# One run of heads beside one run of projections: a two-layer attention trunk with its groups joined

## The chip, the core and the metric

The kernel runs on one core of a Trainium2 chip. The metric is the device time of one execution in microseconds (us); the kernel before took 1171.78 us (median of three runs, 1171.17 to 1171.89). Engines are named as the profile names them: PE multiplies matrices, PEld loads its weights, DVE is the vector engine, ACT the scalar engine, POOL the general one, and SP issues most transfers.

## The reference

The input is 512 tokens of 1024 numbers, float32. There are two layers. Cut to what matters here:

```python
h = rms_norm(x, g_mix[0])
proj = h @ w_in_even             # A: q, k, v of 8 heads; B: q of 8 heads, k and v of 2
a_out = dilated_attention(aq, ak, av, slopes)               # strided windows, three dilations
b_out = sliding_window_sink_attention(bq, bk, bv, sinks, slopes)   # window 128, learned sink
x = x + concat(a_out, b_out) @ w_out_even
x = x + squared_relu_mlp(rms_norm(x, g_mlp[0]), w_up[0], w_down[0])
h = rms_norm(x, g_mix[1])
proj = h @ w_in_odd              # q, k, v of 16 heads C, and a forget logit per head
x = x + forgetting_attention(q, k, v, log_f) @ w_out_odd
x = x + squared_relu_mlp(rms_norm(x, g_mlp[1]), w_up[1], w_down[1])
```

Queries and keys are normed per head (`rms_norm` over 64 numbers). Every head is a causal softmax attention with a bias on the logits.

## The kernel before, in words

**Precision.** Each product of two float32 matrices is made of three matmuls, with both operands split into a high and a low half (`whi`, `wlo` for weights). The split costs an instruction on ACT, POOL or DVE for the high half and one on DVE or POOL for the low half, per 128 x 512 weights.

**Projections.** `project` multiplies the normed input with 256 or 512 columns of the input weights. It runs over the 8 blocks of 128 input rows and the 4 blocks of 128 tokens: 96 matmuls into the four `pj` banks of PSUM (tag `pA`). Then a callback uses the banks. For values `prep_v` scales and splits them. For queries and keys `norm_heads` (L240 to L261) copies each bank (ACT, L247), squares it (ACT, L249), sums by head (DVE, L250), takes a reciprocal root in some 15 small DVE instructions, and multiplies two tiles on DVE and two on POOL (L260). `project` is a generator: it yields after every 12 matmuls, and each yield counts as 64 columns where 512 are projected, 32 where 256 are.

**Heads.** `attend` goes over pairs of heads. For a pair, `prep_q` and `prep_k` transpose the normed tiles on PE (`qkT`, L267) and split them (ACT and DVE, L277, L278, L159, L160); the second half of each K is filled by a transfer that SP issues (L290). `scores` makes four blocks of scores per head (`S`, L325, L326), biases them and takes the row extreme (DVE, L339), exponentiates (ACT, L342) and scales by the reciprocal sum (POOL, or ACT for the last block). `values` transposes the probabilities (`PT`, L362), splits them (ACT L374, DVE L375), multiplies with V (`O`, L382) and adds halves (`yf`, ACT L385, DVE L386). The values of a head are made during the scores of the next one. All these banks share the four of tag `pB`. The generator yields after each block, so that a pair of heads is 19 steps, 14 for the first pair of a layer.

**Output projection.** `out_part` multiplies finished pairs of heads (`ys`) with the output weights (`op`, 12 matmuls and one DVE addition per 128 columns for four pairs). The last two pairs' part is done at the start of the MLP stage, by `finish`.

**What sets the order.** `run` (L430) takes one generator of heads and one of projections and steps the one that lags: projections go when their share of `n_dense` columns is not above the heads' share of `n_att` steps plus a lead. Layer 0 has three such runs: the first four dilated heads (0 to 3) beside the projections of the sliding-window heads; the eight sliding-window heads (4 to 11) beside the projections of the second dilated group; heads 12 to 15 beside two thirds of the output projection. Layer 1 has four runs, of heads 16 to 19, 20 to 23, 24 to 27 and 28 to 31, beside the next group's projections and at last the output projection. `LEADS` holds a lead for each run: 0, 0, -0.16 in layer 0, and 0.33, -0.3, -0.23, -0.09 in layer 1. A run ends only when both of its generators are done. This order is the order of recording; a scheduler then turns it into the order of each engine, moving ready instructions ahead within limits.

## Time and profile before

| | |
|---|---|
| median of three runs | 1171.78 us |
| the profiled execution | 1169.99 us, span 1168.2 us |
| first score of head 0, head 4, head 12, head 15 | 54.22, 107.66, 172.25, 199.03 us |
| first `up` matmul of layer 0's MLP | 227.79 us |
| first score of head 16, head 31 | 627.40, 802.67 us |
| first `up` matmul of layer 1's MLP | 831.05 us |

The profile is of one execution, so its times are compared with its own 1169.99 us, not with the median. Busy time of PE counts every matmul's modelled duration, and these overlap: a matmul of 512 columns is shown with 0.39 us and the next one starts 0.23 us after it. So a wait of PE is best seen as a start that comes late. The granted clock of PE was 1.00 in all stretches that are used here. POOL works in the attention stages alone.

### The profile page before, as it was taken

To read this page: it belongs to the slowest core of one execution; us is meant where nothing else is said; L and a number is where in the kernel's file an instruction comes from. 1 tells how busy PE (TensorE), PEld (TensorE's weight loads), DVE (VectorE), ACT (ScalarE), POOL (GpSimd) and SP (SyncE) were. 2 spreads that over 40 slices of the span, in tenths; PEclk is the share of its full clock that TensorE was granted. 3 is DMA by queue.
4 is the path that set the end of the run, shared out by engine and by line. 5 is a ranking of instruction groups with operands and counts; after the bars stand their busy time and mean duration, and the time that the engine had idled before them with its cause. 6 is when DMAs were issued, how large, how long until landed. Compare 5 with 4: busy or idle time off the path is not lost.

```text
span 1168.2 us, 17496 instructions
## 1 busy us (share of the span) xinstructions
PE 1146.4 (98%) x6256; PEld 981.4 (84%) x6256; DVE 879.8 (75%) x1870; ACT 646.6 (55%) x1349; POOL 203.0 (17%) x296
## 2 busy tenths in 40 slices
PE   8999989999999999999999999999999999999998
PEld 7987878887988988988887888888888888888887
DVE  7878999969947847855647877788858749669676
ACT  6556867655445545444335685656756455465452
POOL 1445434200000000000155445332100000000000
PEclk9999999999999999999999999999999999999999
DMA  7532024132332332333443323343430721623403
GB/s 257 160 91 73 19 73 145 58 123 73 101 117 91 91 108 91 96 121 108 148 127 109 103 89 110 100 124 112 163 106 3 232 91 51 202 73 108 148 34 109
DMA packets 100655, 126.57 MB, mean 108 GB/s; under 512 B 6184, under 2 KB 79944, under 8 KB 100568
## 3 DMA queue, kind: packets, MB, share of 16 engines
q1 hardware_dynamic: 99384, 121.23, 34.0%
q10 hardware_dynamic: 608, 2.13, 0.5%
q0 software_dynamic: 576, 2.10, 0.4%
q8 instruction: 49, 0.80, 0.3%
q14 instruction: 38, 0.31, 0.1%
HBM read 112.29 MB, written 6.32 MB: 102 GB/s over the span
## 4 chain that ended last, share of the span: by engine, by line
PE 82%; DVE 9%; DMA 3%; ACT 2%; POOL 1%; issue 1%; SPq 0%; ACTq 0%; POOLq 0%; DVEq 0%
PE up L164 10%; PE up L167 10%; PE up L168 10%; PE pj L231 4%; PE pj L233 4%; PE pj L232 4%; PE O L382 3%; PE PT L362 2%; PE Y L1023 2%; PE Y L1022 2%; PE Y L1020 2%; PE op L168 2%; PE op L164 2%; PE op L167 2%; PE S L325 2%; DVE wlo L155 1%
## 5 line engine op out<-in xcount | busy, mean ns | idle before, releaser
L164 PE MATMUL up<-xin,whi 128*128 128x512 f32 x512 | 200.5, 392 | 0.0
L168 PE MATMUL up<-xin,whi 128*128 128x512 f32 x512 | 199.3, 389 | 0.0
L167 PE MATMUL up<-xin,wlo 128*128 128x512 f32 x512 | 199.2, 389 | 0.0
L769 ACT CAST whi<-wraw 128x512 fp32r<-128x512 f32 x228 | 139.2, 619 | 105.5 <-PE up L168 47.3
L770 DVE TENSOR_TENSOR wlo<-wraw,whi 128x512 fp32r<-128x512 f32 x228 | 151.7, 686 | 53.7 <-ACT whi L769 53.5
L168 PEld LDWEIGHTS up<-xin,whi 128*128 128x128 f32 x512 | 96.1, 188 | 20.1
L164 PEld LDWEIGHTS up<-xin,whi 128*128 128x128 f32 x512 | 96.1, 188 | 19.9 <-issue 0.2
L167 PEld LDWEIGHTS up<-xin,wlo 128*128 128x128 f32 x512 | 96.2, 188 | 19.7 <-issue 0.2
L342 ACT ACTIVATE P<-P,negm 128x128 f32<-128x128 f32 (+5 forms) x128 | 69.6, 544 | 51.8 <-DVE negm L339 47.9
L231 PE MATMUL pj<-whi,hn 128*128 128x512 f32 (+2 forms) x256 | 88.7, 346 | 0.0
L951 ACT ACTIVATE u<-up 128x512 f32<-128x512 f32 x64 | 38.3, 598 | 90.9 <-PE up L168 90.9
L233 PE MATMUL pj<-whi,hn 128*128 128x512 f32 (+2 forms) x256 | 86.9, 339 | 0.0
L232 PE MATMUL pj<-wlo,hn 128*128 128x512 f32 (+2 forms) x256 | 86.8, 339 | 0.0
L152 POOL TENSOR_SCALAR whi<-wraw 128x512 fp32r<-128x512 f32 x88 | 61.1, 696 | 141.5 <-PE pj L233 121.3
L790 DVE TENSOR_TENSOR t<-u 128x256 f32<-128x256 f32 x56 | 23.2, 424 | 63.3 <-ACT u L1094 61.5
L155 POOL TENSOR_TENSOR wlo<-wraw,whi 128x512 fp32r<-128x512 f32 x48 | 64.4, 1345 | 20.8 <-ACT whi L150 18.1
L231 PE MATMUL pj<-whi,h 128*128 128x512 f32 (+1 forms) x192 | 65.6, 348 | 0.7 <-DVE v L160 0.7
L232 PE MATMUL pj<-wlo,h 128*128 128x512 f32 (+1 forms) x192 | 65.3, 341 | 0.2 <-DVE wlo L155 0.2
L233 PE MATMUL pj<-whi,h 128*128 128x512 f32 (+1 forms) x192 | 65.5, 343 | 0.0
L350 POOL TENSOR_SCALAR P<-P,rden 128x256 f32<-128x256 f32 (+2 forms) x96 | 47.7, 500 | 90.8 <-DVE rden L345 90.1
L155 DVE TENSOR_TENSOR wlo<-wraw,whi 128x512 fp32r<-128x512 f32 (+1 forms) x72 | 49.7, 697 | 17.5 <-POOL whi L152 9.8
L374 ACT CAST PT<-PT 128x256 fp32r<-128x256 f32 (+3 forms) x128 | 49.5, 405 | 19.3 <-PE PT L362 18.5
(229 smaller groups left out, 3051.7 us busy)
## 6 DMA issues: line engine op xcount, KB each, us to landing
wraw<-in_w_up SPq DMA_DIRECT2D x64, 512.0 KB, 4.0
wraw<-in_w_down SPq DMA_DIRECT2D x56, 512.0 KB, 4.2
wraw<-in_w_in_odd SPq DMA_DIRECT2D x36, 256.0 KB, 3.4
mraw<-in_w_down SPq DMA_DIRECT2D x16, 512.0 KB, 4.7
K<-K SPq DMA_DIRECT2D x26, 256.0 KB
wraw<-in_w_in_even SPq DMA_DIRECT2D x10, 512.0 KB, 4.0
wraw<-in_w_in_even SPq DMA_DIRECT2D x16, 256.0 KB, 4.5
xl<-xsp SPq DMA_DIRECT2D x8, 512.0 KB
```

The source lines that it names most:

```text
L152: nc.gpsimd.tensor_scalar(dst_h, src, 1.0, 1.0, op0=OP.mult, op1=OP.mult)
L155: in_order((nc.gpsimd if lo == "pool" else nc.vector).tensor_sub(dst_l, src, dst_h.bitcast(F32)))
L164: m = nc.tensor.matmul(o, wh, xh, start=start, stop=False, skip_group_check=more)
L167: nc.tensor.matmul(o, wl, xh, start=False, stop=False, skip_group_check=more)
L168: nc.tensor.matmul(o, wh, xl, start=False, stop=stop, skip_group_check=more)
L231: nc.tensor.matmul(o, xh, hi[:, :n], start=k == 0, stop=False)
L232: nc.tensor.matmul(o, xh, lo[:, :n], start=False, stop=False)
L233: nc.tensor.matmul(o, xl, hi[:, :n], start=False, stop=k == DC - 1)
L342: nc.scalar.activation(p[:, :ne], p[:, :ne], AF.Exp, scale=-1.0, bias=negm[:, i:i + 1], accum_out=den[:, i:i + 1])
L374: nc.scalar.copy(dst[:, 0], pt[:, :n])
L769: sca(nc.scalar.copy(dst_h, src))
L770: late.append(lambda: vec(nc.vector.tensor_sub(dst_l, src, dst_h.bitcast(F32))))
```

## The change

`run` now takes the heads of a whole layer as one generator and all its projections, with the first parts of the output projection behind them, as another. In place of a share and a lead it has a list of points (heads' steps, projected columns); between points the wanted number of columns is a straight line, and projections go while they are below it. `LEADS`, `NB`, `AHEAD` and `ahead` are gone. `SKEW` is 200: at the end of each group of heads the projections stand 200 columns beyond the point that the group needs; at step 0 they stand 100 columns ahead.

```diff
-LEADS = (0.0, 0.0, -0.16, 0.33, -0.3, -0.23, -0.09)
+SKEW = 200
-NB = 86
@@
-            def run(att, n_att, dense, n_dense, lead=0.0):
+            def run(att, dense, points):
                 a = d = 0
-                while True:
-                    if d / n_dense <= (a + lead * n_att) / n_att or att is None:
+                while att is not None:
+                    (a0, d0), (a1, d1) = next((p, q) for p, q in zip(points, points[1:]) if a < q[0] or q is points[-1])
+                    if dense is not None and d < d0 + (d1 - d0) * (a - a0) / (a1 - a0):
                         c = next(dense, None)
                         if c is None:
-                            break
-                        d += c
+                            dense = None
+                        else:
+                            d += c
+                    elif next(att, "end") == "end":
+                        att = None
                     else:
-                        if next(att, "end") == "end":
-                            att = None
                         a += 1
-                if att is not None:
-                    for _ in att:
+                if dense is not None:
+                    for _ in dense:
                         pass
@@
-                run(att_a(0), 32, chain(kv_b(), project([(1536, 2048)], qk_use("b", 8))), 768, LEADS[0])
-                run(att_b(), NB, chain(qk_a(1), v_a(1)), 768, LEADS[1])
-                run(chain(att_a(1), last_values()), 38, chain(out_part([0, 1, 4, 5], True),
-                                                              out_part([6, 7], False), ahead([2, 3])), 1536, LEADS[2])
+                run(chain(att_a(0), att_b(), att_a(1), last_values()),
+                    chain(kv_b(), project([(1536, 2048)], qk_use("b", 8)), qk_a(1), v_a(1),
+                          out_part([0, 1, 4, 5], True), out_part([6, 7], False)),
+                    [(0, SKEW / 2), (33, 768 + SKEW), (109, 1536 + SKEW), (152, 2930)])
@@
-                for g in range(3):
-                    run(att_c(g), 36, chain(qk_c(g + 1), v_c(g + 1)), 768, LEADS[3 + g])
-                run(chain(att_c(3), last_values()), 42, chain(out_part([0, 1, 2, 3], True),
-                                                              out_part([4, 5], False), ahead([6, 7])), 1536, LEADS[6])
+                run(chain(*[att_c(g) for g in range(4)], last_values()),
+                    chain(*[f(g) for g in range(1, 4) for f in (qk_c, v_c)],
+                          out_part([0, 1, 2, 3], True), out_part([4, 5], False)),
+                    [(0, SKEW / 2), (33, 768 + SKEW), (71, 1536 + SKEW), (109, 2304 + SKEW), (152, 3700)])
```

Every engine has the same instructions before and after, in another order. Three places are shown. The lines of the new kernel stand two lower than those of the old (L231 is L229).

PE where the sliding-window heads begin in layer 0. `pj3_902` (`pj3_863` in the new order) is the last bank of the projection of their queries, `qk_1219` and `qk_1220` (`qk_1179`, `qk_1180`) are its normed tiles, and `S_1329` (`S_1376`) is the first score of head 4. Before:

```order
L233 MATMUL pj3_902<-whi_1159,h0_7_336 128x512
...
L232 MATMUL pj1_1274<-wlo_1463,h0_2_208 128x512
L267 MATMUL qkT_1313<-ident_72,qk_1219 128x128 x2
L233 MATMUL pj1_1274<-whi_1462,h0_2_208 128x512
L231 MATMUL pj2_1275<-whi_1462,h0_2_208 128x512
L267 MATMUL qkT_1313<-ident_72,qk_1220 128x128 x2
...
L325 MATMUL S_1329<-K_1305,Q_1318 128x256
```

And now:

```order
L231 MATMUL pj3_863<-whi_1107,h0_7_336 128x512
L380 MATMUL O_1144<-PT_1063,v0_102 128x512 x2
...
L231 MATMUL pj3_1225<-whi_1304,h0_3_216 128x512
L265 MATMUL qkT_1347<-ident_72,qk_817 128x128 x2
L265 MATMUL qkT_1347<-ident_72,qk_818 128x128 x2
L265 MATMUL qkT_1360<-ident_72,qk_1179 128x128 x2
L265 MATMUL qkT_1360<-ident_72,qk_1180 128x128 x2
L229 MATMUL pj0_1222<-whi_1421,h0_4_273 128x512
```

Between the first row and the first transpose of the normed queries stand 29 matmuls of 512 columns before and 48 now. Ahead of the first score of head 4 stand 30 more of them than before; on DVE one more `wlo`. After the first score of head 15 there are 24 `op` matmuls less.

PE at the first pair of heads of layer 1. `pj3_6624` is the last bank of the projection of the first group's queries and keys, `qk_6765` and `qk_6766` are the normed tiles (two of 128 tokens each: the first of a tile is multiplied on DVE, the second on POOL). Before:

```order
L233 MATMUL pj3_6624<-whi_6737,hn_6410 128x512
L231 MATMUL pj0_6808<-whi_6815,hn_6161 128x512
...
L233 MATMUL pj3_6811<-whi_6854,hn_6284 128x512
L267 MATMUL qkT_6882<-ident_72,qk_6765 128x128 x2
L267 MATMUL qkT_6882<-ident_72,qk_6766 128x128 x2
L267 MATMUL qkT_6892<-ident_72,qk_6765 128x128 x2
L267 MATMUL qkT_6892<-ident_72,qk_6766 128x128 x2
L231 MATMUL pj0_6808<-whi_6909,hn_6325 128x512
```

And now:

```order
L231 MATMUL pj3_6624<-whi_6737,hn_6410 128x512
L229 MATMUL pj0_6808<-whi_6815,hn_6161 128x512
...
L231 MATMUL pj3_6811<-whi_6819,hn_6203 128x512
L265 MATMUL qkT_6847<-ident_72,qk_6765 128x128 x2
L265 MATMUL qkT_6857<-ident_72,qk_6765 128x128 x2
L229 MATMUL pj0_6808<-whi_6888,hn_6244 128x512
L265 MATMUL qkT_6847<-ident_72,qk_6766 128x128 x2
L265 MATMUL qkT_6857<-ident_72,qk_6766 128x128 x2
```

Between the first row and the first transpose stand 48 matmuls before and 24 now. After the transposes 24 matmuls of the projection follow until the first score, as before.

DVE at the same place, from the end of that norm (`rs_6789`) to the K of the first pair. Before:

```order
L134 SCALAR_TENSOR_TENSOR rs_6789<-rsq_6791,rsq_6790 128x32
L260 TENSOR_TENSOR qk_6765<-qk_6765,rs_6789 128x512
L260 TENSOR_TENSOR qk_6766<-qk_6766,rs_6789 128x512
L155 TENSOR_TENSOR wlo_7136<-wraw_7129,whi_7135 128x512
L278 TENSOR_TENSOR Q_6887<-qkT_6882,Q_6887 64x512
L160 SCALAR_TENSOR_TENSOR K_6897<-qkT_6892,gg_84,K_6897 64x512
```

And now:

```order
L258 TENSOR_TENSOR qk_6765<-qk_6765,rs_6789 128x512
L258 TENSOR_TENSOR qk_6766<-qk_6766,rs_6789 128x512
L276 TENSOR_TENSOR Q_6852<-qkT_6847,Q_6852 64x512
L158 SCALAR_TENSOR_TENSOR K_6862<-qkT_6857,gg_84,K_6862 64x512
L276 TENSOR_TENSOR Q_6852<-qkT_6847,Q_6852 64x512
L158 SCALAR_TENSOR_TENSOR K_6866<-qkT_6857,gg_84,K_6866 64x512
L153 TENSOR_TENSOR wlo_7185<-wraw_7178,whi_7184 128x512
```

The split of a weight block stood ahead of the first `Q` and now stands behind the last `K`.

## The prediction

> **What bounds the kernel now.** I read the page first, then busy time by stage, then who waits for whom on the tensor engine (PE) and on the vector engine (DVE), and at last single rows at the places where the change moves work. The page and three stretches (from the first matmul on scores of head 4 to the first `up` matmul of layer 0; the first MLP; from the first score of head 16 to the first `up` of layer 1):

> ```profile
> PE 1146.4 (98%) x6256; PEld 981.4 (84%) x6256; DVE 879.8 (75%) x1870; ACT 646.6 (55%) x1349; POOL 203.0 (17%) x296
> ...
> core 0: us, PE busy (x) PEld busy (x) DVE busy (x) ACT busy (x) POOL busy (x), PEclk, DMA share, GB/s
> 107.66:227.79 120.13, 115.58 (x682) 97.79 (x681) 111.33 (x309) 84.88 (x225) 48.22 (x90) 1.00 0.25 75
> 227.79:558.00 330.21, 327.12 (x1914) 290.46 (x1913) 236.92 (x432) 169.80 (x307) 0.31 (x1) 1.00 0.33 100
> 627.40:831.05 203.65, 201.77 (x1233) 172.59 (x1234) 162.71 (x436) 131.26 (x314) 82.49 (x110) 1.00 0.39 115
> ```

> PE is busy 98% of the span, so waits of PE are all there is to win: the work itself is the same in both kernels. The DVE column tells the two attention stages apart. In layer 0 from head 4 on DVE works 111.33 of 120.13 us (93%); in layer 1 it works 162.71 of 203.65 us (80%). So the second half of layer 0's attention has two limits that lie close together, layer 1's has PE alone. Who waits there (first PE, then DVE in the layer 0 stretch, then PE in layer 1 from 602 to 831 us; columns: who, for whom, us in total, times, longest):

> ```profile
> PE S L325 <- DVE Q L278: 1.8, 2, 1.5
> PE S L325 <- DVE yf L386: 1.8, 2, 1.6
> PE PT L362 <- DVE negm L339: 0.5, 2, 0.3
> PE op L168 <- DVE y L155: 0.3, 1, 0.3
> ...
> DVE yf L386 <- ACT yf L385: 3.3, 4, 1.2
> DVE acc L481 <- PE op L168: 1.2, 3, 0.6
> DVE wlo L155 <- POOL whi L152: 0.7, 1, 0.7
> DVE P L339 <- PE S L326: 0.6, 3, 0.3
> DVE rden L345 <- ACT P L342: 0.5, 2, 0.3
> DVE ss L250 <- ACT sq L249: 0.3, 1, 0.3
> DVE wlo L770 <- ACT whi L769: 0.2, 1, 0.2
> ...
> PE S L325 <- DMA K<-K: 2.6, 3, 1.2
> PE O L382 <- DVE PT L375: 0.3, 1, 0.3
> PE O L382 <- ACT PT L374: 0.2, 1, 0.2
> ```

> In layer 0 every wait of PE ends with DVE, and DVE itself waits for PE only 1.2 + 0.6 = 1.8 us in 120. That is the sign that DVE, not PE, sets the pace there.

> **Part 1, the seam between the first dilated group and head 4.** Today the projection of the sliding-window queries ends too close to its use:

> ```profile
> 103.15 0.39 PE L232 MATMUL pj<-wlo,h 128*128 128x512 f32 x1
> 104.40 0.41 PE L267 MATMUL qkT<-ident,qk 128*128 128x128 f32 x2 [0.86 <-DVE qk L260]
> 104.57 0.48 PE L233 MATMUL pj<-whi,h 128*128 128x512 f32 x1
> 104.88 0.40 PE L231 MATMUL pj<-whi,h 128*128 128x512 f32 x1
> 105.76 0.44 PE L267 MATMUL qkT<-ident,qk 128*128 128x128 f32 x2 [0.48 <-DVE qk L260]
> 107.20 0.39 PE L231 MATMUL pj<-whi,h 128*128 128x512 f32 x1
> 107.43 0.39 PE L232 MATMUL pj<-wlo,h 128*128 128x512 f32 x1
> 107.66 0.31 PE L325 MATMUL S<-K,Q 128*128 128x256 f32 x1
> ```

> Undisturbed 512-column matmuls start 0.227 us apart (107.20 to 107.43 to 107.66), whatever their shown duration. So the first transpose is late by 104.40 - 103.15 - 0.23 = 1.02 us and the third by 105.76 - 104.88 - 0.23 = 0.65 us: 1.67 us at the seam. Between the end of that projection and the first of these transposes the order has 29 matmuls of 512 columns before and 48 now, and work of head 3 beside them: 19 x 0.227 = 4.3 us more, against the 1.0 us that is missing. What covers it is the next projection's first matmuls. This seam goes: -1.7 us for head 4's start. Bounds: -1.7 and 0 (0 if the ready time of the norm moves as well).

> **Part 2, what follows head 4 in layer 0.** The order shows 30 more 512-column projection matmuls on PE ahead of head 4's first score than before, and on DVE one more `wlo` (0.69 us in the row below), no more. So PE does 30 x 0.227 = 6.8 us of work earlier, DVE 0.7 us. Head 4 then starts at 107.66 + 6.81 - 1.67 = 112.8 us. From there PE has 6.8 us less to do and DVE 0.7 us less.

> ```profile
> 108.18 0.69 DVE L155 TENSOR_TENSOR wlo<-wraw,whi 128x512 fp32r<-128x512 f32 x1 [0.65 <-POOL whi L152]
> ...
> 227.79 0.39 PE L164 MATMUL up<-xin,whi 128*128 128x512 f32 x1
> ```

> If PE set the pace with the waits it has now, the rest would take 120.13 - 6.81 = 113.3 us and the MLP would start at 226.1 us, 1.7 us earlier. If DVE sets it, the rest takes 111.33 - 0.69 = 110.6 us plus DVE's idle time. That idle time is 120.13 - 111.33 = 8.8 us now. With all of it left the MLP starts at 232.2 (+4.4 us); with none of it at 223.4, and then PE's bound of 226.1 holds (-1.7). I take 6.2 us: the 1.8 us in which DVE waited for PE go, since PE has less to do, and one of the four waits of `yf` for the scalar engine (0.8 us of 3.3) goes, since a DVE that is behind meets fewer of them. The rest are waits for ACT and POOL and gaps between rows that the new order does not touch. That gives 112.8 + 110.6 + 6.2 = 229.6, or +1.8 us. What stalls where: with 24 matmuls less after head 15's first score, PE has less to do while DVE finishes, and waits in `S`, `PT` and `op`. If PE, not DVE, should turn out to pace this stretch, the same move is worth the 1.7 us.

> **Part 3, the start of layer 1.** Before, the first group ran with a lead of 0.33 x 768 = 253 columns; now the first point is 100 columns. In matmuls: between the last one of the first query/key projection and the first transpose of its normed result stand 48 before, 24 now. The norm behind that projection, and what follows it:

> ```profile
> 609.19 0.59 ACT L247 COPY qk<-pj 128x512 f32<-128x512 f32 x1 [0.27 <-PE pj L233]
> 615.60 2.15 DVE L260 TENSOR_TENSOR qk<-qk,rs 128x512 f32<-128x512 f32 x2
> 615.72 2.93 POOL L260 TENSOR_TENSOR qk<-qk,rs 128x512 f32<-128x512 f32 x2 [3.12 <-DVE rs L134]
> 619.65 0.40 PE L233 MATMUL pj<-whi,hn 128*128 128x512 f32 x1
> 619.88 1.04 PE L267 MATMUL qkT<-ident,qk 128*128 128x128 f32 x8
> 621.22 1.09 DVE L155 TENSOR_TENSOR wlo<-wraw,whi 128x512 fp32r<-128x512 f32 x1 [3.47 <-POOL whi L152]
> 622.34 0.69 DVE L278 TENSOR_TENSOR Q<-qkT,Q 64x512 fp32r<-64x512 f32 x1
> 625.79 0.39 PE L232 MATMUL pj<-wlo,hn 128*128 128x512 f32 x1
> 627.40 0.35 PE L325 MATMUL S<-K,Q 128*128 128x256 f32 x1 [1.23 <-DMA K<-K]
> ```

> Today 48 x 0.227 = 10.9 us separate the two, so the projection's last matmul left PE at 619.88 - 10.90 = 608.98, and POOL's last product is ready at 615.72 + 2.93 = 618.65: 9.7 us, hidden with 1.2 us to spare. DVE, ACT and POOL run this norm in the same order in the new kernel. With 24 matmuls PE comes to the transposes at 608.98 + 5.45 = 614.43. Eight transposes (0.11 us apart: 1.04 us for eight, the last of which is shown with some 0.27) and one matmul between them would end at 615.5; the last three now cannot start before 618.65 and end at 619.0. PE stands for 3.5 us, and nothing can slip in, since behind these transposes the order is fixed. Part of it comes back: today `wlo` (1.09 us) stands on DVE ahead of the first `Q`, and the first score is late by 627.40 - 625.79 - 0.23 = 1.38 us; in the new order that `wlo` stands behind `Q` and `K`. Net +2.1 us; bounds +3.5 (the wait for K stays) and 0 (the norm runs quicker than in the trace).

> **Part 4, the rest of layer 1.** PE's listed waits there besides that first one are 2.6 - 1.2 + 0.5 = 1.9 us. The projections were already far ahead at the other three seams, so these seams cost nothing that shows. Where the norms now fall on other heads, such waits can go or come: 1.9 us less to 2 us more. I take half of the listed ones, -0.9 us. SP's queue has the same 138 rows in the order before and after; a weight load that is issued earlier finds the DMA engines 25% to 40% busy by the windows above. The MLPs and the time before head 0 have the same instructions; costed at 0.

> **The sum** against the profiled execution's own 1169.99 us (span 1168.2): +1.8 (layer 0) + 2.1 (layer 1's start) - 0.9 = +3.0, so 1173.0. The median of the three timed runs is 1171.78, 1.8 us above that execution; on it, 1174.8 us.

> **The rivals.**

> *PE stays the limit in layer 0 (faster).* The seam's 1.7 us go, and of the two long waits of scores for `Q` and `yf` (1.5 and 1.6 us, 3.1 together) half, -1.6; layer 1 gives +2.1 - 1.9 = +0.2. Sum -3.1: 1168.7 us. For it: PE is the busier engine by the page. Against it: the MLP would start at 227.8 - 3.3 = 224.5 us, which leaves DVE 224.5 - 112.8 - 110.6 = 1.1 us of idle time where it has 8.8 now, 3.3 of them waits for ACT. It decides from the point where DVE idles less than 2.7 us between head 4 and the MLP; at 4.4 us layer 0 is even.

> *It evens out (no change).* DVE idles 4.4 us there, layer 0 gives 0, layer 1 gives +2.1 - 0.9: +1.2, 1173.0 us. This is also what comes if the streams only change places: the same work on every engine, and at the first group of layer 1 fewer columns ahead, not more.

> *The long stand slows PE's clock (slower still).* The longest stand of PE in the attention and MLP stages today is 2.4 us, and the clock stays at 1.00 in that stretch:

> ```profile
> 288.84 0.28 PE L1073 MATMUL Z<-b,whi 128*128 128x256 f32 x1
> 291.50 0.39 PE L1069 MATMUL Y<-t,whi 128*128 128x256 f32 x1 [2.38 <-DVE acc L1085]
> ```

> The new one is 3.5 us, broken by a few transposes. If the clock then fell to half for as long, matmuls of 1.75 us would be lost: 1174.8 + 1.7 = 1176.5 us. Against it: five transposes and a matmul fall into the stand. [...]

> **How the numbers follow.** A change of 0.2% is 2.3 us, about what a measurement of this kernel can tell from none. Forecast (DVE paces layer 0, the norm is uncovered in layer 1): 0.48 at 1174.8. Evens out: 0.28 at 1173.0. Faster: 0.17 at 1168.7. Clock: 0.07 at 1176.5. Of the forecast's share 0.06 lies below +2.3 us. So faster 0.18 (0.17 and a little of the even case), same 0.33, slower 0.49. The likeliest case alone spans 1172.5 to 1180 (layer 0 from +0.5 to +4.4, layer 1 from 0 to +3.5). The range has to take in most of the faster case as well: 1168.7 to 1179.5.

> **What would show it.** Right: PE waits about 3 us in `qkT` on the norm some 8 us before the first score of layer 1; no wait for `qk` before head 4; DVE busy over 93% from head 4 to the first `up`, which starts at 228 to 231 us. Wrong: DVE idle under 3 us there with the MLP starting before 227; or `qkT` in layer 1 without a wait. The prediction falls if waits of PE in layer 1's middle grow by more than 2 us, where DVE has room by the 80%, or if the MLPs move at all.

## The result, and the profile after

The changed kernel took 1192.64 us (median of four runs, 1191.25 to 1193.39) against 1171.65 us of the kernel before beside it: a ratio of 1.0178 with an interval of 1.0161 to 1.0196. It is slower, as forecast, but by 21 us and not by 3: 1192.6 lies outside the range of 1168.7 to 1179.5 us. The profiled execution took 1193.39 us, its span is 1191.6.

The same three stretches as before (first score of head 4 to the first `up`; the first MLP; head 16 to the second `up`), from the table by stretches:

```profile
core 0: us, PE busy (x) PEld busy (x) DVE busy (x) ACT busy (x) POOL busy (x), PEclk, DMA share, GB/s
119.63:240.07 120.44, 112.42 (x651) 93.23 (x650) 109.57 (x305) 82.96 (x223) 44.86 (x86) 0.97 0.24 72
240.07:577.23 337.16, 334.27 (x1940) 296.94 (x1939) 241.54 (x440) 172.62 (x314) 0.31 (x1) 0.99 0.33 99
639.31:854.45 215.14, 209.82 (x1257) 177.72 (x1255) 164.47 (x437) 132.04 (x314) 84.90 (x113) 0.99 0.37 110
```

Two things are to be seen. The first stretch is as long as before (120.44 to 120.13 us), although PE has some 7 us less to do in it. And the granted clock is no longer 1.00. Busy time of PE hides both, so I used another measure: each matmul is given the step at which the next one starts when nothing disturbs it (0.227 us for 512 columns, 0.176 for 384, 0.120 for 256, 0.109 for a transpose), and what the starts come later than that is called **lateness** here. By stage:

| | before: length, late | after: length, late | more |
|---|---|---|---|
| first matmul to head 0 | 52.2, 6.6 | 58.9, 9.0 | 2.4 |
| heads 0 to 3 | 53.4, 4.0 | 58.7, 6.8 | 2.8 |
| heads 4 to 14 | 91.4, 9.4 | 90.2, 9.8 | 0.4 |
| head 15 to the first `up` | 28.8, 1.0 | 30.2, 7.7 | 6.8 |
| first `up` to head 16 | 399.6, 7.1 | 399.2, 11.7 | 4.6 |
| head 16 to the second `up` | 203.7, 8.3 | 215.1, 14.8 | 6.5 |
| all, with 0.3 in the second MLP | 36.7 | 60.1 | 23.4 |

The spans differ by 1191.6 - 1168.2 = 23.4 us: the loss is all late starts. (Ahead of head 0 kernels with the same instructions differ by 2 us in the runs below, so the first row is partly chance.) Where PE waited (who, for whom, us in total, times, longest), in heads 0 to 3, from head 4 to `up`, from there to head 16, and from head 16 on:

```profile
PE O L380 <- ACT PT L372: 1.8, 2, 1.2
PE O L380 <- DVE PT L373: 1.5, 2, 0.8
...
PE op L165 <- DVE wlo L153: 5.3, 4, 4.0
...
PE Y L1065 <- DVE acc L1081: 2.4, 1, 2.4
PE qkT L265 <- DVE qk L258: 1.8, 1, 1.8
PE qkT L265 <- POOL qk L258: 1.1, 2, 0.6
...
PE S L323 <- DMA K<-K: 3.9, 2, 2.5
PE S L323 <- DVE rsq L128: 0.9, 1, 0.9
```

And the stretches in which the granted clock was below 1 (column PEclk; there were none before, except behind the last matmul):

```profile
109.69:113.10 3.41, 3.41 (x9) 2.73 (x10) 1.28 (x2) 0.58 (x1) 1.09 (x3) 0.50 0.11 32
225.74:232.57 6.83, 4.84 (x11) 3.80 (x12) 3.40 (x6) 1.24 (x2) 0.19 (x1) 0.50 0.54 164
304.25:307.66 3.41, 3.41 (x19) 3.41 (x18) 3.37 (x9) 0.62 (x1) 0.00 (x0) 0.50 0.55 154
631.93:635.34 3.41, 3.41 (x10) 2.84 (x11) 2.29 (x4) 2.62 (x5) 1.74 (x2) 0.50 0.00 0
778.70:782.11 3.41, 3.41 (x17) 2.61 (x16) 2.10 (x9) 2.64 (x9) 1.44 (x3) 0.50 0.07 14
```

Each is one or two times 3.41 us long and stands behind waits listed above. Summed over the matmuls in them, the slower steps cost 1.5, 2.4, 1.4, 1.5 and 1.5 us: 8.3 of the 23.4 us. The other 15 us are late starts at full clock.

The longest one, at the end of layer 0, in PE's, DVE's and POOL's rows:

```profile
222.09 0.84 PE L162 MATMUL op<-y,whi 128*128 128x512 f32 x3
223.22 0.50 PE L162 MATMUL op<-y,whi 128*128 128x512 f32 x1 [0.29 <-DVE acc L482]
227.73 0.80 PE L165 MATMUL op<-y,wlo 128*128 128x512 f32 x1 [4.01 <-DVE wlo L153]
228.32 0.63 PE L166 MATMUL op<-y,whi 128*128 128x512 f32 x1
...
223.08 1.72 DVE L766 TENSOR_TENSOR wlo<-wraw,whi 128x512 fp32r<-128x512 f32 x1
224.73 1.74 DVE L153 TENSOR_TENSOR y<-yf,y 128x512 fp32r<-128x512 f32 x1
226.40 0.68 DVE L766 TENSOR_TENSOR wlo<-wraw,whi 128x512 fp32r<-128x512 f32 x1
227.00 1.28 DVE L153 TENSOR_TENSOR wlo<-wraw,whi 128x512 fp32r<-128x512 f32 x2
...
222.99 2.94 POOL L153 TENSOR_TENSOR wlo<-wraw,whi 128x512 fp32r<-128x512 f32 x2
```

PE has nothing but the last output part left. The low half of its weights stands on DVE behind two splits of MLP weights and the split of the last heads' `y`; in the kernel before its two blocks stood 12 and 9 rows ahead of that `y`. While POOL splits (222.99 to 225.93 us), two of these DVE instructions take 1.72 and 1.74 us; the next, of the same shape, takes 0.68. No run here takes POOL's work away, so it is not shown that POOL is what slows them.

The late `wlo` is only half of it. In the kernel before, the last split that PE waited for was that of `y` (DVE, then PE):

```profile
217.01 1.29 DVE L155 TENSOR_TENSOR y<-yf,y 128x512 fp32r<-128x512 f32 x1
218.36 0.73 PE L168 MATMUL op<-y,whi 128*128 128x512 f32 x2 [0.30 <-DVE y L155]
```

It was ready 19.3 us after head 15's first score (217.01 + 1.29 - 199.03), and PE waited 0.3 us. The `wlo` of the change is ready 17.8 us after it (227.00 + 0.68 - 209.88), 1.5 us sooner, and PE waits 4.0 us. What changed more is PE's own work from head 15 to `up`: length less lateness is 28.8 - 1.0 = 27.8 us before and 30.2 - 7.7 = 22.5 us now, 5.3 us less, by the 24 `op` matmuls that are already done. 5.3 less 1.5 is 3.8 us, about what the wait grew by (4.0 - 0.3).

### The profile page after: what moved, and what is told of

Its sections match the earlier page's. It is cut to its first block, busy times and chain, and to the rows that moved or that the text cites. A ratio compares the mean times of both kernels' runs of the same rounds, so it can differ in the third digit from the quotient of the medians.

```text
span 1191.6 us, 17503 instructions
## 1 busy us (share of the span) xinstructions
PE 1160.5 (97%) x6256; PEld 990.0 (83%) x6256; DVE 881.5 (74%) x1870; ACT 646.9 (54%) x1349; POOL 202.7 (17%) x296
## 4 chain that ended last, share of the span: by engine, by line
PE 81%; DVE 12%; issue 2%; ACT 2%; POOL 1%; DMA 1%; SPq 0%; POOLq 0%; DVEq 0%; ACTq 0%
PE up L162 10%; PE up L165 10%; PE up L166 10%; PE pj L229 4%; PE pj L230 4%; PE pj L231 4%; PE O L380 2%; PE op L165 2%; PE op L166 2%; PE PT L360 2%; PE op L162 2%; PE Y L1019 2%; PE Y L1018 2%; PE Y L1016 2%; PE Y L1065 1%
## 5 line engine op out<-in xcount | busy, mean ns | idle before, releaser
L229 PE MATMUL pj<-whi,hn 128*128 128x512 f32 (+2 forms) x256 | 89.5, 350 | 0.0
L231 PE MATMUL pj<-whi,hn 128*128 128x512 f32 (+2 forms) x256 | 87.3, 342 | 0.0
L150 POOL TENSOR_SCALAR whi<-wraw 128x512 fp32r<-128x512 f32 x88 | 58.6, 668 | 149.3 <-PE pj L231 127.5
L229 PE MATMUL pj<-whi,h 128*128 128x512 f32 (+1 forms) x192 | 66.9, 355 | 1.0 <-DVE v L158 0.7
L231 PE MATMUL pj<-whi,h 128*128 128x512 f32 (+1 forms) x192 | 65.8, 344 | 0.0
L165 PE MATMUL op<-y,wlo 128*128 128x512 f32 x128 | 52.9, 413 | 5.3 <-DVE wlo L153 5.3
```

Source lines behind the costliest of these rows:

```text
L150: nc.gpsimd.tensor_scalar(dst_h, src, 1.0, 1.0, op0=OP.mult, op1=OP.mult)
L165: nc.tensor.matmul(o, wl, xh, start=False, stop=False, skip_group_check=more)
L229: nc.tensor.matmul(o, xh, hi[:, :n], start=k == 0, stop=False)
L231: nc.tensor.matmul(o, xl, hi[:, :n], start=False, stop=k == DC - 1)
```

## The experiments

Times are against the kernel before, timed beside each (1171.46, 1171.73 and 1171.87 us).

**One layer at a time.** `l0_joined` has the change in layer 0 and the old runs and leads in layer 1; `l1_joined` is the reverse.

```diff
 l0_joined, layer 1 (l1_joined: the same with layer 0's three old runs)
-run(chain(*[att_c(g) for g in range(4)], last_values()), ...)
+for g in range(3):
+    run_old(att_c(g), 36, chain(qk_c(g + 1), v_c(g + 1)), 768, LEADS[3 + g])
+run_old(chain(att_c(3), last_values()), 42, ..., 1536, LEADS[6])
```

> Layer 0 in one run as in the change; layer 1 in the four old runs with the old leads. Theory (new stands of PE, and a clock window at half speed behind each long one): of the 23.4 us by which PE's starts came later than their nominal steps in the change, 2.4 lie before head 0, 2.8 in heads 0 to 3, 0.4 in heads 4 to 14 and 6.8 between head 15 and the first up: +12.3 us on the kernel before, 1184 us (1186 if the 2.4 us stand in the first MLP again falls into one clock window). The stand before the first up is there again with two windows at half clock. Rival (the clock drops come from somewhere else, and the move of columns costs what the prediction had): +1.8 us, 1173.5 us, and drops at other places than behind stands.

> Layer 0 in the three old runs, layer 1 in one run as in the change. Theory: layer 1's start +2.9 to +4.6 us (a stand of 3.4 us less the old wait for K, a window at half clock, and one more in the MLP by chance), heads 16 to 28 +6.4 us: +9.3 to +11.0, 1181 to 1183 us. Rival (layer 1 costs what the prediction had, +1.2 us, and its late K's come from what layer 0 left behind): 1173 us.

1181.74 us (1.0083, 1.0068 to 1.0098) and 1182.34 us (1.0091, 1.0074 to 1.0108). The two add up: +10.3 and +10.9 us make 21.2, and the whole change costs 21. The first lies below the 1184 us expected, which was worked out from the 23.4 us between the two profiles; between the medians there are 21. In layer 1 the old runs have 7.5 us of lateness from head 16 on, the joined one 14.5. The stands came back to the tenth: 4.28 us ahead of `up` with two slow windows in `l0_joined`, 3.4 us at layer 1's start with one in `l1_joined`. In `l1_joined` the second late K (2.50 us) had no slow window behind it, in the change it had; that is taken up below.

**Two stands, by points.**

```diff
-[(0, SKEW / 2), (33, 768 + SKEW), (109, 1536 + SKEW), (152, 2930)]
+[(0, SKEW / 2), (33, 768 + SKEW), (109, 1536 + SKEW), (152, 2690)]
-[(0, SKEW / 2), (33, 768 + SKEW), ...     (layer 1)
+[(0, 253), (33, 768 + SKEW), ...
```

> The change with two points moved: layer 0's last point 2690 columns in place of 2930 (so that some 24 to 36 more output matmuls are left behind the last heads), layer 1's first point 253 in place of 100 (48 matmuls again between the projection and its transposes). Theory (these stands are a lack of other matmuls for PE): the stand of 4.3 us at the end of layer 0 and its two slow windows go, -6.8 us; the stand at layer 1's start and its window go, -2.9 us: 1183 us. Rival (the weights of the last output part are late on DVE whatever PE does): PE stands over 3 us there again, only layer 1's start is won: 1189.7 us.

1187.03 us (1.0129, 1.0114 to 1.0144). Half of the theory fell. Layer 1's start: the waits of `qkT` and the slow window are gone, K is late by 1.38 us as before the change. The end of layer 0: nothing moved. The same 72 `op` matmuls stand behind head 15's first score (96 before the change), and PE waits 4.0 us for the same `wlo`. The scheduler pulls ready output matmuls ahead whatever the points say, so this experiment could not tell a lack of work from late weights. (The time is 2.7 us below the 1189.7 us expected if only layer 1's start is won; in the profile 1.7 us of that lie in heads 0 to 3, where the slow window did not come.)

**The late weights.** The first weights of the last part are loaded and split between the two earlier parts:

```diff
+def ahead(pairs):
+    tiles[0] = out_weights(pairs, 0)
+    yield 0
-out_part([0, 1, 4, 5], True), out_part([6, 7], False)),
+out_part([0, 1, 4, 5], True), ahead([2, 3]), out_part([6, 7], False)),
```

> The change, with the first weights of layer 0's last output part loaded and split between the two earlier parts, so that their low halves stand on DVE some 50 rows ahead of the split of the last heads' y and not behind it. Theory (PE's stand of 4.3 us ahead of the first up is DVE being late with these low halves, behind two splits of MLP weights and the last y, and its two slow clock windows follow from the stand): the stand falls under 1.5 us, no slow window there, the stretch from head 15 to up loses 5 to 7 us of excess: 1186 us. Rival (PE simply has no work left there, and the last y is as late as the weights): the stand stays over 3 us, now on y, 1192 us.

1186.29 us (1.0122, 1.0107 to 1.0137), the time that the theory had. From head 15 to `up` the lateness falls from 7.7 to 1.0 us at a clock of 1.00:

```profile
206.89:233.60 26.71, 26.49 (x134) 21.59 (x133) 24.62 (x52) 18.25 (x38) 5.06 (x6) 1.00 0.21 69
```

1.7 us of it come back in heads 12 to 14, where PE now waits for `acc`, `negm` and K. But the place of these two rows on DVE is not shown to be the cause by this. The scheduler also left more for PE to do: 85 `op` matmuls stand behind head 15's first score in place of 72, and PE's own work from there to `up` is 26.7 - 1.0 = 25.7 us against 22.5. These 3.2 us cover most of the 4.0 us; the last split, now that of `y`, is ready 17.2 us after head 15 in place of 17.8.

**The clock by itself.** PE gets 38 transposes that nothing reads, where it stood:

```diff
+if finish is not None and li == 0 and c == 0:
+    fb = bank("pB", "fill")
+    for n in range(38):
+        tc.keep_in_program_order(nc.tensor.transpose(fb[:, :P], ident, ident))
```

> The change with 38 transposes of the identity into a free bank (4.1 us of PE work that nothing reads) where PE stands at the end of layer 0. What waits for DVE there waits as long as before. Theory (the clock falls because PE stood, and the slow windows cost 3.4 us there): no slow window between 223 and 235 us, the stretch from head 15 to up is 2.5 to 3.4 us shorter although PE has more to do: 1189.7 us. Rival (the clock falls for another reason, or the half clock costs nothing because DVE sets the pace there): same length within 0.7 us, 1192 to 1193 us.

1189.13 us (1.0148, 1.0132 to 1.0163). There is no slow window between 219 and 236 us. PE's rows:

```profile
219.11 4.31 PE L476 MATMUL fill<-ident 128*128 128x128 f32 x38
223.18 0.48 PE L162 MATMUL op<-y,whi 128*128 128x512 f32 x1
224.79 0.50 PE L165 MATMUL op<-y,wlo 128*128 128x512 f32 x1 [1.13 <-DVE wlo L153]
```

The awaited `wlo` comes as long after head 15 as it did (17.9 us in both kernels: 224.79 - 206.87 and 227.73 - 209.88). From there to `up` it takes 10.8 us for 47 matmuls, against 12.3 us for 44. So it was PE's idle time that lowered the clock here, and the low clock cost 2.3 us (12.34 less 44 x 0.227). And the wait itself fell from 4.0 to 1.1 us with `wlo` as late as before, because PE had 4.1 us more to do. So the stand is as much a lack of other work as a late split, which is the theory of `tail_start`, whose edit did not reach it. The stretch became shorter by 1.5 us and not by 2.5 to 3.4: I had counted half of both slow windows, but PE stood through 2.0 us of the first, and three matmuls more came behind the wait. The rest of the 3.5 us of the median lies at other places: in the profile the slow windows of head 3 and of the first MLP are missing too.

**Where the norm falls in layer 1.** Every pair of heads has a chain of transposes, Q, K and a transfer of K; every group has a norm. In the change, at head 26 (DVE, SP, PE), and in the kernel before at the seam ahead of head 24 (DVE, and PE's work from 704.5 to 713.1 us):

```profile
770.66 2.14 DVE L258 TENSOR_TENSOR qk<-qk,rs 128x512 f32<-128x512 f32 x2
772.84 0.68 DVE L276 TENSOR_TENSOR Q<-qkT,Q 64x512 fp32r<-64x512 f32 x1
775.77 0.76 DVE L158 SCALAR_TENSOR_TENSOR K<-qkT,gg,K 64x512 fp32r<-64x512 f32 x1
774.32 2.74 SPq L288 DMA_DIRECT2D K<-K  x2
777.33 0.36 PE L323 MATMUL S<-K,Q 128*128 128x256 f32 x1 [2.51 <-DMA K<-K]
```

```profile
707.21 2.14 DVE L260 TENSOR_TENSOR qk<-qk,rs 128x512 f32<-128x512 f32 x2
714.44 0.68 DVE L278 TENSOR_TENSOR Q<-qkT,Q 64x512 fp32r<-64x512 f32 x1
...
L233 PE MATMUL pj<-whi,hn 128*128 128x256 f32 x24 | 6.8, 283 | 0.0
L231 PE MATMUL pj<-whi,hn 128*128 128x256 f32 x24 | 6.8, 283 | 0.0
L232 PE MATMUL pj<-wlo,hn 128*128 128x256 f32 x24 | 6.8, 283 | 0.0
```

In the old order the end of the norm ran beside 72 projection matmuls without heads; in the new one it stands on DVE straight ahead of a pair's Q and K. Three tests. First, the norm behind that pair:

```diff
-[(0, SKEW / 2), (33, 768 + SKEW), (71, 1536 + SKEW), (109, 2304 + SKEW), (152, 3700)]
+[(0, SKEW / 2), (33, 768 + 80), (71, 1536 + 80), (109, 2304 + 80), (152, 3700)]
```

> The change with layer 1's three middle points at 80 columns ahead in place of 200, so that the next group's norm is recorded behind the Q and K of a group's second pair and not ahead of them. Theory (the norm's DVE chain of 7 us stands ahead of Q and K on DVE, so K is late and PE stands): the waits for K of 1.5 and 2.7 us and the slow window behind the second go, heads 16 to 28 are back near the excess of the kernel before: -6.4 us, 1186 us. Rival (the transfer of K itself is late, because of other transfers): the waits for K stay within 1 us of what they are, 1192 to 1193 us.

1192.56 us (1.0178, 1.0162 to 1.0193): no gain. Both waits for K, at heads 22 and 26, are gone, so the order on DVE caused them and not the transfer. But their time came back elsewhere. Who PE waits for there now (the K in the list is another, at head 30):

```profile
PE PT L360 <- DVE PT L373: 2.3, 2, 1.2
PE PT L360 <- DVE negm L337: 1.5, 2, 1.2
PE S L323 <- DMA K<-K: 1.5, 1, 1.5
```

Second, a piece of projections without heads in the middle of each group:

```diff
+[(0, SKEW / 2), (24, 512), (24.01, 768), (62, 1280), (62.01, 1536), (100, 2048), (100.01, 2304), (152, 3700)]
```

> The change with other points in layer 1: in each group the values' 256 columns follow in one piece behind the 512 columns of queries and keys (a jump of 256 columns at step 24, 62, 100), in the middle of the group and not at its end. Theory (a group's norm is some 10 us of DVE; the old order hid it under a stretch of projections without heads at the end of each run, and joining the groups takes that stretch away, so that the norm stands in the way of the heads wherever it falls): with such a stretch again the excess of heads 16 to 31 falls from 14.4 us to about 8 as in the kernel before: -6 us, 1186.5 us. Rival (what costs is that the norm lies inside a group and not at its end): over 12 us of excess there, 1191 us or more.

1190.13 us (1.0160, 1.0141 to 1.0179), with 12.8 us of lateness from head 16 on: the expected gain did not come. The piece was there (at head 22, 93 projection matmuls in a row from 715.5 to 728.0 us). But the norm had begun ahead of it: one of its sums of squares stands on DVE in front of the pair's first score, and PE waits for that score's extreme (DVE, then PE):

```profile
709.82 0.67 DVE L248 TENSOR_REDUCE ss<-sq 128x8 f32<-128x512 f32 x1
710.53 0.29 DVE L337 CUSTOM_DVE_ANT_0 P<-S,bias 128x128 f32<-128x128 f32 x1
...
710.88 0.55 PE L360 MATMUL PT<-ident,P 128*128 128x128 f32 x3 [1.57 <-DVE negm L337]
```

So by this run alone the rival stands: a norm inside a group costs. Whether it is the norm at all, the third test tells.

Third, the norms left out, in both orders:

```diff
-st["qk", key] = norm_heads(outs, nh, *sq)
+st["qk", key] = norm_heads(outs, nh, *sq, skip=li == 1 and key in (1, 2, 3))
```

> Layer 0 in the old runs, layer 1 in one run as in the change, and the norm of queries and keys left out for the last three groups of layer 1 (they are copied only; 5 of some 13 DVE and ACT operations per bank stay). To be read against the kernel before with the same left out. Theory (joining costs in heads 16 to 31 because the three norms then lie among the heads' own DVE work, where PE has no stretch of projections without heads to cover them): without norms the two kernels' excess from head 16 to the second up differs by less than 2 us (6.4 us apart with norms), and the whole time by the start of layer 1 alone, 3 to 5 us. Rival (the other order of columns itself, late transfers of K, or the tail of the heads costs): over 4 us apart in that stretch.

> The kernel before with the same three norms of layer 1 left out. Theory (the old order hides these norms under projections without heads): hardly faster than with them, 0 to 2 us: 1170 to 1171.7 us. Rival (the norms cost the old order as much): 4 us or more faster.

1175.30 us (1.0036, 1.0022 to 1.0050) and 1170.14 us (0.9987, 0.9977 to 0.9996). Without these norms the joined order has 6.4 us of lateness from head 16 on and the old order 5.9; with them 14.5 and 8.3. So the norms cost the joined order 8 us and the old one 2.4, and of the 6.2 us between the orders 0.5 are left. So what layer 1 lost from head 16 on hangs on the norms. The two medians are still 5.2 us apart; in the profiles 3.9 us of that lie between the first `up` and head 16, at layer 1's start. That the seams covered the norms, because DVE did them there while PE had work that needed no head, is how the rows of the one seam above read; `jump_mid`, meant to give such a cover back, did not win it back, and a piece placed so that it covers a whole norm in the middle of a group was not tried.

**Joined, but not ahead.**

```diff
-SKEW = 200
+SKEW = 40
```

> The change with SKEW 40 in place of 200: the groups joined, the projections hardly ahead. Theory (joining is what costs in layer 1, the 200 columns ahead cost at the end of layer 0, where they leave 24 output matmuls less): the stand at the end of layer 0 goes (-6.8 us), the late start of head 0 and the waits for O in heads 2 and 3 go or change places (-2 to -4), layer 1's start stands longer (12 matmuls in place of 24: +2.7), heads 16 to 31 keep an excess over 12 us: 1182 to 1186 us. Rival (the 200 columns ahead are the whole cost): 1172 to 1175 us.

1186.72 us (1.0121, 1.0099 to 1.0142), just above the time expected. The stand at the end of layer 0 is gone, with 94 `op` matmuls again behind head 15's first score, and layer 1 keeps its cost (17.1 us of lateness from head 16 on), as the theory had it. Not expected: heads 4 to 11 have 4.4 us of lateness (7.5 before the change), and a new stand comes at head 14, with two slow windows behind it. SP's rows and PE's:

```profile
187.04 2.52 SPq L842 DMA_DIRECT2D wraw<-in_w_up  x2
189.61 2.43 SPq L288 DMA_DIRECT2D K<-K  x2
...
197.20 0.55 PE L323 MATMUL S<-K,Q 128*128 128x256 f32 x1 [3.98 <-DMA K<-K]
```

Two loads of MLP weights (512 KB each) were issued just ahead of the K that the scores wait for. That suggested layer 0 alone, hardly ahead, with points that keep the old order of K and MLP weights on SP, and a second choice of points beside it. Both have layer 1's old runs:

```diff
-[(0, SKEW / 2), (33, 768 + SKEW), (109, 1536 + SKEW), (152, 2930)]
+[(0, 20), (33, 808), (109, 1576), (152, 2800)]     l0_near
+[(0, 20), (33, 798), (109, 1556), (152, 2930)]     l0_near2
```

> Layer 0 in one run, the projections only 40 columns ahead at the ends of groups and 20 at the start, last point 2800; layer 1 in the old runs. In the kernel with SKEW 40 heads 4 to 11 had 3.1 us less excess than before, and one stand of 4.1 us on a late K of head 14, whose transfer stood behind two loads of MLP weights on SP; here the order on SP has K ahead of them as in the kernel before. Theory (layer 0 can be joined without loss if no stand comes of it): 1168.5 to 1170.5 us. Rival (joining moves the waits elsewhere in layer 0 too): 1173 us or more.

> The same with other points: 30 columns ahead at the end of the first group, 20 at the end of the sliding-window heads, last point 2930. Its DVE order among the sliding-window heads is that of the kernel before. Theory: like the kernel before within 1.5 us, 1170 to 1173 us. Rival (joining costs in layer 0 whatever the points): 1175 us or more.

`l0_near`: 1167.98 us (0.9972, 0.9961 to 0.9984), faster than both kernels and 0.5 us below what was expected. `l0_near2`: 1171.23 us (1.0000, 0.9991 to 1.0009). From head 4 to `up` in `l0_near`, with PE's waits there:

```profile
107.93:225.84 117.91, 115.35 (x685) 98.95 (x685) 108.03 (x309) 85.06 (x225) 46.68 (x91) 1.00 0.25 78
...
PE O L382 <- ACT PT L374: 1.5, 1, 1.5
PE O L382 <- DVE PT L375: 0.9, 2, 0.5
```

The old waits of scores for `Q` and `yf` (3.6 us) are gone, 2.4 us of others stand there. Joining is no loss in layer 0 when no stand comes of it; `l0_near2` lost the gain again to a wait of 3.2 us for K at head 12.

## Why the prediction was wrong

**What bounds the kernel.** Right: the work is the same, and waits of PE are what counts. What was missing is that a wait can cost more than its length: at five places here 1.4 to 2.4 us more.

**Part 1, the seam before head 4.** No wait for `qk` is left there, as forecast. But the term of -1.7 us took no account of where the norm goes instead: into heads 2 and 3, where PE waits 0.6 and 1.2 us in `O` for the splits of `PT`, with a slow window behind (1.5 us). Up to head 4 the change was forecast at -1.7 us and cost 5.2, and 2.4 of that lie ahead of head 0. The slow window is chance of the grid (last section): in `tail_start`, `tail_wlo`, `fill_tail` and `jump_mid`, with the same instructions up to there, it did not come, and heads 0 to 3 have 5.1 to 5.5 us of lateness in place of 6.8.

**Part 2, the rest of layer 0.** Forecast +3.5 us of lateness from head 4 on (116.8 us in place of 113.3), measured +7.1. The step that failed is that DVE sets the pace of the whole stretch, and in its sum the 6.2 us of idle time left to DVE. DVE's work was right (109.6 us for 110.6), but it idled 120.4 - 109.6 = 10.9 us and was busy 91%, not over 93%. The 1.8 us in which it waited for PE did not go: they became 6.2 us (3.7 + 2.2 + 0.3), the 3.7 in the additions that wait for the output matmuls. Heads 4 to 14 are as late as before within 0.4 us; all the loss is one stand at the end. The prediction named it in half a sentence ("PE has less to do while DVE finishes, and waits in `S`, `PT` and `op`"), and there it was right: the 24 matmuls less are most of the stand, as the rows of `y` and `fill_tail` show. It did not price it as a stand, with 2.4 us of half clock behind it.

**Part 3, the start of layer 1.** The mechanism was right to the tenth: 3.4 us of waits in `qkT` (1.92 + 0.79 + 0.72) against 3.5 forecast, and the wait for K gone. Mis-sized by the slow window behind them, 1.5 us. That made +4.6 us from `up` to head 16, with 1.4 us of another slow window, in an MLP that was costed at 0.

**Part 4, the rest of layer 1.** Forecast -0.9 us, measured +6.5 (of them 1.5 clock). This step was wrong in its reading: "The projections were already far ahead at the other three seams, so these seams cost nothing that shows." By the rows above they cost little because the norms ran beside them. The bound of 2 us more came from the waits that were there, and the pair without norms shows that the norms account for 5.6 of the 6.2 us between the orders. By the signs that it gave itself the prediction falls here: PE's listed waits in layer 1's middle grew from 1.9 to 5.1 us, and the first MLP moved.

**The rivals.** The clock had a chance of 0.07 and one place of 1.75 us. That it would fall to half for as long as PE stands was an estimate: no attention or MLP stage of the kernel before shows a drop. The drop came at five places, at 0.50 for 3.41 us (6.83 at one of them), with 1.4 to 2.4 us each. "It evens out" and "PE stays the limit" fell with the change; the second has its point in `l0_near`, where the two long waits it spoke of do go.

**The sum** was +3.0: -1.7, +3.5, +2.1 and -0.9. Measured: +5.2, +7.1, +4.6 and +6.5, together 23.4. Every term was short by 2.5 to 7.4 us, and 8.3 us of the miss are the clock. The range was built from bounds of single waits; none held that several waits in the same few microseconds also slow what follows.

## What to carry to other kernels

Before a seam is taken away, look at what runs on the other engines during it: a stretch in which the busiest engine works alone may be the only cover of a long serial chain elsewhere. When work is moved, follow the chain that depends on it to the place where it now lands, and look at what is queued behind it on its engine. Before work is moved ahead of a last dependent step, compare what PE has left with the time at which the other engine is done: the difference is the stand. And price a stand of PE over 2 us at its length plus 0 to 2.4 us more, as it was here.

## What the runs showed of the hardware

```profile
300.84:304.25 3.41, 1.03 (x9) 0.83 (x9) 3.41 (x5) 0.62 (x1) 0.00 (x0) 1.00 0.00 0
...
294.93:298.34 3.41, 1.97 (x17) 1.76 (x15) 3.41 (x3) 1.24 (x2) 0.00 (x0) 1.00 0.30 102
298.34:301.76 3.42, 2.48 (x20) 2.49 (x21) 3.38 (x10) 0.62 (x1) 0.00 (x0) 1.00 0.44 136
```

The same holds for the late K of head 26, 2.5 us in both kernels, first in the change (where the slow stretch from 778.70 us, listed above, follows) and then in `l1_joined`:

```profile
775.29:778.70 3.41, 1.37 (x12) 1.31 (x12) 2.81 (x8) 0.98 (x4) 0.00 (x0) 1.00 0.66 139
...
764.97:768.38 3.41, 2.04 (x17) 1.83 (x18) 2.58 (x9) 1.07 (x4) 0.28 (x1) 1.00 0.55 115
768.38:771.79 3.41, 3.41 (x27) 3.05 (x26) 3.41 (x11) 3.21 (x11) 1.75 (x4) 1.00 0.03 10
```

So the 2.38 us of the kernel before, at a clock of 1.00, which the prediction shows at the rival of the slower clock, say little: in the change and in `before_nonorm` a slow stretch stood behind the same wait.
